# Loads of the state-space parameters by 32 partitions, and modulations of the up stage as fp32 matmuls by quarters

## The chip, the cores and the metric

The kernel runs on one core of a Trainium2 chip. Its five engines each work through their own list of instructions in order: TensorE (PE; PEld are its weight loads), VectorE (DVE), ScalarE (ACT), GpSimd (POOL) and SyncE (SP), which here issues nearly all DMAs. The metric is the device time of one execution in microseconds; the median of three runs stands for a kernel. One further execution is profiled, and all rows below come from it.

## The reference, cut to what matters

Two layers work on 512 latent and 256 context tokens of width 1024. Layer 0 mixes by attention, layer 1 by a state-space recurrence; a convolutional feed-forward network follows each.

```
m = split(silu(c) @ w_mod[i] + b_mod[i], 6)        # w_mod[i]: 1024 x 6144, all fp32
h = rms_norm(x, g_pre) * (1 + m[1]) + m[0]         # shift and scale, also before the FFN
x = x + m[2] * rms_norm(mixer(h), g_post)          # gate
dt = exp(log_step); lb = exp(lam * dt)             # per direction, group (64) and state (64)
bb = ((lb - 1) / lam) * b                          # b: 64 x 16 complex numbers per group
a = conv3(h @ w_up); ffn = (silu(gate) * val) @ w_down      # w_up: 1024 x 5632
```

The modulations m are needed once for c (latent) and once for c_ctx (context): two rows of 1024 numbers per unit, where a unit is one of the six parts of one layer.

## The kernel before, in words

Products of the model run on TensorE in three passes, high times high, high times low and low times high (`mm3`, lines 145 to 147). So each weight tile of 128x1024, loaded by SP into one of five raw buffers, is split: ScalarE makes the high half (line 108), VectorE the low one (line 109). `Weights` loads the tiles in the order of a plan; a raw buffer comes free when its reader has done with it. Instructions are ordered on each engine by a scheduler that works on its own estimate of times, so the order on an engine is not that of the source.

Attention (about 165 to 385 us) runs beside two other things. The modulations of two groups are summed on TensorE, with the weights read from their raw buffers (`mods_mm`, line 227, 32x512 outputs). And `ssm_tables` makes the tables of the state-space layer: it loads lambda, the log step and B with `by_dg` (line 1105), two loads of 64 partitions for each parameter, then the signs (128 numbers, line 1120), and VectorE negates these (`sg2`, line 1122) for the last table. The exponential of the log step (`exp`, lines 1071 to 1082) is small work on VectorE.

The up stage of layer 0 (`ffn_up`, about 445 to 890 us) takes 22 pairs of w_up tiles. Per pair TensorE fills PSUM banks (`up`), ScalarE applies one tap of the convolution (line 870) and VectorE two (line 874), which frees the banks. Beside this, VectorE builds the state-space matrices (PT and QT, lines 1243 to 1245) that TensorE transposes (pP, line 1262) or multiplies (pK, line 1291) into one of two PSUM banks with the tag "aux". And `mods_ahead` makes five units of layer 1's modulations, eight w_mod tiles each: with c as the factor of a partition, VectorE multiplies and adds into an SBUF sum (lines 297, 299), or ScalarE multiplies (line 293) and GpSimd adds (line 295). At the end of a unit TensorE sums over partitions with a matrix of ones (line 306). The first two units are made for latent and context tokens, the other three for latents alone. The sixth unit is made in the same way in the up stage of layer 1 (`ffn1`, about 1395 to 1530 us).

Of the kernel before, what the change touches and what calls it, by code (L numbers as in the profile page):

```python
# [9 lines left out]
FT = mybir.dt.float32  # L10
# [9 lines left out]
P = 128  # L20
D = 1024
# [110 lines left out]
class Kernel:  # L132
# [137 lines left out]
    def mods_ahead(self, psum, pool, units, lcs):  # L270
# [3 lines left out]
        ones = pool.tile([P, 32], FT, name="ones")  # L274
        nc.gpsimd.memset(ones, 1.0)
        n = 64 * lcs
        for l, grp, m in units:
            b = self.small.tile([P, 512], FT, name="mbias", tag="mbias", bufs=1)[:n]
            g = self.small.tile([P, 512], FT, name="mgain", tag="mgain", bufs=1)[:n]
            name = {(0, 1): "g_pre_mix", (1, 0): "g_post_mix", (2, 0): "g_pre_ffn", (2, 1): "g_post_ffn"}.get((grp, m))  # L280
            for lc in range(lcs):
                c = slice(64 * lc, 64 * lc + 64)
                nc.sync.dma_start(b[c], dap(I["b_mod"], l * 6144 + grp * 2048 + m * D, [[512, 2], [0, 32], [1, 512]]))
                if name:
                    nc.sync.dma_start(g[c], dap(I[name], l * D, [[512, 2], [0, 32], [1, 512]]))
            accs = [pool.tile([P, D], FT, name=f"macc{i}", tag=f"macc{i}", bufs=1) for i in range(lcs)]
            for k in range(KD):
                w = self.W.take()
                for lc in range(lcs):
                    a, c = accs[lc], self.cT[:, k, lc:lc + 1]  # L290
                    if lc == lcs - 1 and (lc or k % 2):
                        o = w if k else a
                        nc.scalar.activation(o, w, AF.Copy, scale=c)  # L293
                        if k:
# [7 lines left out]
            p = psum.tile([P, 512], FT, name="pm", tag="aux", bufs=2)  # L302
            for lc in range(lcs):
                for j in range(2):
                    q = 64 * lc + 32 * j
                    nc.tensor.matmul(p[q:q + 32], ones, accs[lc][:, j * 512:(j + 1) * 512], start=True, stop=True)
            v.tensor_tensor(b, p[:n], b, op=OP.add)
# [6 lines left out]
            for lc in range(lcs):  # L314
                nc.gpsimd.dma_start(dap(self.mdram[l, grp], lc * 2048 + m * D, [[512, 2], [1, 512]]),
                                    b[64 * lc:64 * lc + 64:32, :])
            if l and (grp, m) in ((1, 1), (2, 0)):
                p = psum.tile([P, 4, P], FT, name="pmc", tag="aux", bufs=2)
                for i in range(4):
                    nc.tensor.transpose(p[:, i, :64], b[:, i * P:(i + 1) * P], self.ident[:64, :64])  # L320
                v.tensor_copy(self.cols[1, 1][:, 0, grp - 1, :].rearrange("p (q b) -> p q b", b=4),
                              p[:, :, 0:33:32].rearrange("p b q -> p q b"))
# [643 lines left out]
    def ffn0(self):  # L966
# [25 lines left out]
        def mods():  # L992
            for i, units in enumerate(UP_MODS[0]):
                mp = self.pool(f"mods{i}", "right")
                for j, _ in enumerate(self.mods_ahead(ps, mp, units, 2 - i)):
                    if j == KD * len(units) - 1:
                        mp.release()
                    yield
# [821 lines left out]
```

## Time and profile before

| what | value |
|---|---|
| median of three runs | 1720.65 us (1717.9 to 1722.14) |
| profiled execution, its time | 1725.43 us |
| profiled execution, its span | 1723.6 us |
| busy: PE, DVE, ACT, POOL | 1531.6, 1132.2, 776.6, 252.3 us |
| mean granted clock of TensorE | 0.951 |

The span runs from the first instruction to the last; the time is 1.8 us more. Busy time is the union of an engine's instructions. The granted clock is given as a share of full speed: 0.5 is 1.2 GHz and 1.0 is 2.4 GHz. A matmul of fp32 operands leaves two records in the trace, one of the split operands leaves one. Matmuls are pipelined, so the step from one start to the next, not the duration, is what one costs in a stream.

### The profile page before, as it was taken

Reading aid. Unit: us, or ns where it says so; the run is one execution under the profiler, and the core shown is the slowest. Engines: PE = TensorE matmul, PEld = TensorE weight load, DVE = VectorE, ACT = ScalarE, POOL = GpSimd, SP = SyncE. Lnnn points to the kernel's source line nnn. Section 1 sums busy time; section 2 is a strip of 40 time slices with the busy share of each in tenths; the row PEclk is TensorE's granted clock in tenths of the full one; section 3 lists DMA queues with packets and bytes.
Section 4 is the critical chain, followed back from the end, with each engine's and each line's share of the span. In section 5 each row is a group of like instructions: output and inputs, shape, how many; then the busy total and the mean of one; then the engine's idle time right before and its main releaser. Section 6 shows DMA issues by size and latency. Waiting matters only on the chain.

```text
span 1723.6 us, 22808 instructions
## 1 busy us (share of the span) xinstructions
PE 1531.6 (89%) x8376; PEld 1230.2 (71%) x8376; DVE 1132.2 (66%) x2084; ACT 776.6 (45%) x1470; POOL 252.3 (15%) x203
## 2 busy tenths in 40 slices
PE   5999389999899898988999989673789999999997
PEld 2775258888778777866788877433578888888886
DVE  4653378758988988887863367689835656565334
ACT  4464167756544343332333345565544534443322
POOL 0111050000130402020200010448311001100000
PEclk8999599999999999999999999896899999999999
DMA  9424162158355647585754278664443334432421
GB/s 302 138 75 149 72 208 68 50 182 277 103 174 155 175 142 203 146 206 157 214 133 150 96 244 252 174 187 156 132 151 104 117 98 147 135 94 96 166 74 49
DMA packets 218483, 256.38 MB, mean 149 GB/s; under 512 B 19420, under 2 KB 169572, under 8 KB 217732
## 3 DMA queue, kind: packets, MB, share of 16 engines
q1 hardware_dynamic: 217940, 254.85, 48.8%
q8 instruction: 66, 1.08, 0.3%
q14 instruction: 45, 0.37, 0.1%
q0 software_dynamic: 384, 0.07, 0.0%
q10 hardware_dynamic: 48, 0.01, 0.0%
HBM read 216.95 MB, written 34.80 MB: 146 GB/s over the span
## 4 chain that ended last, share of the span: by engine, by line
PE 64%; DVE 16%; DMA 10%; ACT 5%; issue 3%; SPq 3%; POOL 0%; DVEq 0%; ACTq 0%; POOLq 0%
PE up L145 8%; PE up L146 8%; PE up L147 8%; PE dn L146 5%; PE dn L145 5%; PE dn L147 5%; DMA wraw<-in_w_mod 2%; PE acc L145 2%; PE acc L146 2%; PE acc L147 2%; DMA tab<-tabd 2%; DVE whl L109 2%; PE glu L145 2%; PE glu L147 1%; PE glu L146 1%
## 5 line engine op out<-in xcount | busy, mean ns | idle before, releaser
L109 DVE TENSOR_TENSOR whl<-wraw,whl 128x1024 fp32r<-128x1024 f32 x202 | 259.8, 1291 | 178.3 <-ACT whl L108 176.8
L108 ACT ACTIVATE whl<-wraw 128x1024 fp32r<-128x1024 f32 x206 | 216.9, 1056 | 203.2 <-PE dn L147 137.8
L145 PE MATMUL up<-b,whl 128*128 128x256 f32 (+1 forms) x728 | 248.5, 343 | 27.8 <-DVE h L874 15.9
L146 PE MATMUL up<-b,whl 128*128 128x256 f32 (+1 forms) x728 | 246.7, 340 | 0.1
L147 PE MATMUL up<-b,whl 128*128 128x256 f32 (+1 forms) x728 | 246.4, 340 | 0.0
L145 PEld LDWEIGHTS up<-b,whl 128*128 128x128 f32 x728 | 140.8, 194 | 51.8 <-issue 31.1
L146 PE MATMUL dn<-whl,hs 128*128 128x512 f32 x440 | 171.8, 393 | 4.8 <-DVE whl L109 4.7
L147 PE MATMUL dn<-whl,hs 128*128 128x512 f32 x440 | 170.9, 392 | 0.0
L145 PE MATMUL dn<-whl,hs 128*128 128x512 f32 x440 | 170.3, 392 | 0.5 <-ACT hs L934 0.5
L146 PEld LDWEIGHTS up<-b,whl 128*128 128x128 f32 x728 | 141.1, 194 | 18.9 <-issue 4.3
L147 PEld LDWEIGHTS up<-b,whl 128*128 128x128 f32 x728 | 141.0, 194 | 16.7 <-issue 2.4
L146 PE MATMUL up<-c,whl 128*128 128x512 f32 (+1 forms) x384 | 142.5, 373 | 0.1
L147 PE MATMUL up<-c,whl 128*128 128x512 f32 (+1 forms) x384 | 141.8, 371 | 0.0
L145 PE MATMUL up<-c,whl 128*128 128x512 f32 (+1 forms) x384 | 139.4, 372 | 1.0 <-DVE c L355 1.0
L295 POOL TENSOR_TENSOR macc<-macc,wraw 128x1024 f32<-128x1024 f32 x30 | 81.1, 2704 | 312.1 <-ACT wraw L293 246.2
L874 DVE SCALAR_TENSOR_TENSOR ga<-up,cw,ga 128x511 f32<-128x511 f32 (+1 forms) x132 | 86.3, 655 | 60.3 <-ACT ga L870 59.3
L870 ACT ACTIVATE ga<-up,cw 128x512 f32<-128x512 f32 (+1 forms) x66 | 46.5, 705 | 139.0 <-PE up L147 133.3
L146 PEld LDWEIGHTS dn<-whl,hs 128*128 128x128 f32 x440 | 82.6, 188 | 24.3 <-DVE whl L109 6.5
L874 DVE SCALAR_TENSOR_TENSOR h<-up,cw,h 128x511 f32<-128x511 f32 (+1 forms) x132 | 86.2, 653 | 19.0 <-ACT h L870 18.5
L145 PEld LDWEIGHTS dn<-whl,hs 128*128 128x128 f32 x440 | 82.7, 188 | 18.9 <-ACT hs L934 0.9
L147 PEld LDWEIGHTS dn<-whl,hs 128*128 128x128 f32 x440 | 82.7, 188 | 17.9
L145 PEld LDWEIGHTS up<-c,whl 128*128 128x128 f32 x384 | 71.4, 188 | 15.1 <-DVE c L355 1.5
(358 smaller groups left out, 3151.3 us busy)
## 6 DMA issues: line engine op xcount, KB each, us to landing
wraw<-in_w_up SPq DMA_DIRECT2D x88, 512.0 KB
wraw<-in_w_mod SPq DMA_DIRECT2D x80, 512.0 KB
wraw<-in_w_down SPq DMA_DIRECT2D x66, 512.0 KB
wraw<-in_w_o SPq DMA_DIRECT2D x24, 512.0 KB
Pt<-Pd SPq DMA_DIRECT2D x24, 512.0 KB
Pt<-Qd SPq DMA_DIRECT2D x32, 384.0 KB
wm<-in_w_mod SPq DMA_DIRECT2D x16, 512.0 KB
Pd<-Pb SPq DMA_DIRECT2D x16, 512.0 KB
```

The source lines that it names most:

```text
L108: nc.scalar.activation(w[:, 0], r, AF.Copy)
L109: e.tensor_tensor(w[:, 1], r, w[:, 0], op=OP.subtract)
L145: nc.tensor.matmul(out, a[0], b[0], start=start, stop=False)
L146: nc.tensor.matmul(out, a[0], b[1], start=False, stop=False)
L147: nc.tensor.matmul(out, a[1], b[0], start=False, stop=stop)
L295: nc.gpsimd.tensor_tensor(a, a, o, op=OP.add)
L870: nc.scalar.activation(o, acc, AF.Identity, scale=c[:, 1:2], bias=c[:, 3:4])
L874: nc.vector.scalar_tensor_tensor(x, acc[:, a + s:b + s], c[:, tap:tap + 1], x, op0=OP.mult, op1=OP.add)
```

## The change

The loads of `by_dg` are cut by direction, so that each covers 32 partitions with one run per partition. The log step is loaded first, then lambda, the signs and B. The negation of the signs is written beside the rows that use it. In `mods_ahead`, the sums on VectorE, ScalarE and GpSimd give way to fp32 matmuls: for each w_mod tile, four matmuls whose moving operand is a quarter of 256 columns and whose output lies in one of the four groups of 32 partitions of one PSUM bank ("aux"), which is held through the eight tiles. Bias and gain are loaded by quarters too. The pools for the SBUF sums go.

```
-        for h in range(2):
-            nc.sync.dma_start(t[64 * h:64 * h + 64], dap(I[name], 32 * h * n, [[G * n, 2], [n, 32], [1, n]]))
+            for d in range(2):
+                p0 = 64 * h + 32 * d
+                nc.sync.dma_start(t[p0:p0 + 32], dap(I[name], (G * d + 32 * h) * n, [[n, 32], [1, n]]))
...
+        self.by_dg(ls, "ssm_log_step", 1)
         self.by_dg(lam[:, 0], "ssm_lambda_re", NS)
         self.by_dg(lam[:, 1], "ssm_lambda_im", NS)
-        self.by_dg(ls, "ssm_log_step", 1)
+        nc.sync.dma_start(sg, self.I["signs"])
         self.by_dg(bt[:, 0].rearrange("p n c -> p (n c)"), "ssm_b_re", NS * GC)
         self.by_dg(bt[:, 1].rearrange("p n c -> p (n c)"), "ssm_b_im", NS * GC)
-        nc.sync.dma_start(sg, self.I["signs"])
-        v.tensor_scalar(sg2, sg, -1.0, None, op0=OP.mult)
...
         self.A = self.cst.tile([P, 2, 64], FT, name="lamT")
+        v.tensor_scalar(sg2, sg, -1.0, None, op0=OP.mult)
...
+            for q in range(4):
+                c = slice(32 * q, 32 * q + 32)
+                nc.sync.dma_start(b[c], dap(I["b_mod"], ... + 256 * q, [[0, 32], [1, 256]]))
+            acc = psum.tile([P, 512], FT, name="macc", tag="aux", bufs=2)[:, :256]
             for k in range(KD):
                 w = self.W.take()
-                for lc in range(lcs):
-                    a, c = accs[lc], self.cT[:, k, lc:lc + 1]
-                    if lc == lcs - 1 and (lc or k % 2):
-                        nc.scalar.activation(o, w, AF.Copy, scale=c)
-                        nc.gpsimd.tensor_tensor(a, a, o, op=OP.add)
-                    elif k == 0:
-                        v.tensor_scalar(a, w, c, None, op0=OP.mult)
-                    else:
-                        v.scalar_tensor_tensor(a, w, c, a, op0=OP.mult, op1=OP.add)
+                for q in range(4):
+                    nc.tensor.matmul(acc[32 * q:32 * q + 32], self.cT[:, k, :], w[:, 256 * q:256 * q + 256],
+                                     start=(k == 0), stop=(k == KD - 1))
-            for lc in range(lcs):
-                for j in range(2):
-                    nc.tensor.matmul(p[q:q + 32], ones, accs[lc][:, j * 512:(j + 1) * 512], start=True, stop=True)
```

The order on SP before, in the attention stage: the loads of the parameters, with the gain of the feed-forward norm ahead of them and the signs last.

```order
L220 DMA mgain<-in_g_post_ffn 64x1x512
L1105 DMA lam<-in_ssm_lambda_re 64x1x64 x2
L1105 DMA lam<-in_ssm_lambda_im 64x1x64 x2
L1105 DMA ls<-in_ssm_log_step 64x1x1 x2
L1105 DMA bt<-in_ssm_b_re 64x1x1024
L215 DMA mbias<-in_b_mod 128x1x512
L1105 DMA bt<-in_ssm_b_re 64x1x1024
L1105 DMA bt<-in_ssm_b_im 64x1x1024 x2
L1120 DMA sg<-in_signs 128x1
```

The same place on SP in the changed kernel:

```order
L220 DMA mgain<-in_g_post_ffn 64x1x512
L1086 DMA ls<-in_ssm_log_step 32x1 x4
L1086 DMA lam<-in_ssm_lambda_re 32x64 x4
L1086 DMA lam<-in_ssm_lambda_im 32x64 x2
L215 DMA mbias<-in_b_mod 128x1x512
L1086 DMA lam<-in_ssm_lambda_im 32x64 x2
L1099 DMA sg<-in_signs 128x1
L1086 DMA bt<-in_ssm_b_re 32x1024 x4
L1086 DMA bt<-in_ssm_b_im 32x1024 x4
```

The signs moved from behind the four loads of B to a place ahead of eight; 13 issues stand between the gain and the signs, in place of 11.

On VectorE before, in the same stage, the first exponential (edt), a row maximum of attention (sm) and the negation of the signs (sg):

```order
L1079 SCALAR_TENSOR_TENSOR edt<-edt 128x1
L652 TENSOR_SCALAR sm<-sm 128x1
L1079 SCALAR_TENSOR_TENSOR edt<-edt 128x1 x3
L1122 TENSOR_SCALAR sg_2149<-sg 128x1
L1080 TENSOR_SCALAR edt<-edt 128x1
L1082 TENSOR_TENSOR edt<-edt,eidt 128x1
L655 RECIPROCAL sm<-sm 128x1
```

On VectorE in the changed kernel:

```order
L634 TENSOR_REDUCE sm<-s 128x1
L1058 SCALAR_TENSOR_TENSOR edt<-edt 128x1
L1164 TENSOR_SCALAR sg_2669<-sg 128x1
L1132 RECIPROCAL dz<-dz 128x64
L635 TENSOR_SCALAR sm<-sm 128x1
L1058 SCALAR_TENSOR_TENSOR edt<-edt 128x1
L1059 TENSOR_SCALAR edt<-edt 128x1
```

Though the source has the negation far below, the scheduler puts it at nearly the same place, two small operations earlier.

On TensorE before, in the up stage of layer 0, the end of the second unit: the sums with ones (pm) between two passes of products (up).

```order
L145 MATMUL up<-b_7_3591,whl_5278 128x256
L146 MATMUL up<-b_7_3591,whl_5278 128x256
L147 MATMUL up<-b_7_3591,whl_5278 128x256
L306 MATMUL pm<-macc_4825,ones 32x512 x2
L306 MATMUL pm<-macc_4826,ones 32x512 x2
L146 MATMUL up<-b_2_3578,whl_5486 128x512
```

On TensorE in the changed kernel, earlier in the same stage, the quarters (macc) of two w_mod tiles, the second one torn, and one half of a job's transposes (pP):

```order
L147 MATMUL up<-b_7_3593,whl_4938 128x512
L287 MATMUL macc<-wraw_4941,cT 32x256 x4
L287 MATMUL macc<-wraw_5059,cT 32x256 x3
L1243 MATMUL pP<-ident,PT 128x128 x4
L145 MATMUL up<-b_0_3586,whl_5109 128x512
```

The fourth quarter of wraw_5059 stands 75 rows further on. Before, nothing of the modulations stood on TensorE but the sums with ones, and a job's eight transposes stood together in most places; now they stand in fours while a unit holds its bank.

## Rows read from the trace of the kernel before

**Rows 1.** Stretches: us, busy us (count) by engine, clock, DMA share, GB/s

```profile
175.00:190.00 15.00, 10.29 (x39) 8.03 (x37) 6.07 (x34) 5.65 (x15) 1.57 (x5) 0.55 0.21 68
190.00:210.00 20.00, 0.03 (x1) 0.00 (x0) 0.21 (x2) 0.00 (x0) 0.00 (x0) 0.63 0.12 48
210.00:260.00 50.00, 42.56 (x257) 28.04 (x258) 38.23 (x93) 29.71 (x58) 24.05 (x34) 0.91 0.60 184
445.00:890.00 445.00, 405.03 (x2431) 333.68 (x2430) 375.28 (x515) 175.03 (x274) 75.57 (x35) 0.97 0.60 167
1395.00:1530.00 135.00, 135.00 (x596) 110.82 (x595) 81.04 (x97) 56.73 (x71) 10.22 (x5) 1.00 0.43 127
```

**Rows 2.** Timeline of VectorE: start, us, instruction, idle before and its releaser

```profile
184.06 0.15 DVE L1071 TENSOR_SCALAR edt<-ls 128x1 f32<-128x1 f32 x1 [4.50 <-DMA ls<-in_ssm_log_step]
...
209.79 0.15 DVE L1122 TENSOR_SCALAR sg<-sg 128x1 f32<-128x1 f32 x1 [22.18 <-DMA sg<-in_signs]
```

**Rows 3.** Timeline of SP's DMA issues from 174 to 196

```profile
174.12 0.54 SPq L220 DMA_DIRECT2D mgain<-in_g_pre_ffn  x1
...
176.58 3.16 SPq L1105 DMA_DIRECT2D lam<-in_ssm_lambda_im  x2
179.79 2.60 SPq L1105 DMA_DIRECT2D ls<-in_ssm_log_step  x2
182.49 0.50 SPq L1105 DMA_DIRECT2D bt<-in_ssm_b_re  x1
...
191.02 4.73 SPq L1120 DMA_DIRECT2D sg<-in_signs  x1
```

**Rows 4.** Groups by line in 445:890: busy us, mean ns, idle before, releasers

```profile
L145 PE MATMUL up<-b,whl 128*128 128x512 f32 (+1 forms) x664 | 231.1, 350 | 27.8 <-DVE h L874 15.9 <-DVE ga L874 10.9 <-ACT Pb L1263 0.9
...
L109 DVE TENSOR_TENSOR whl<-wraw,whl 128x1024 fp32r<-128x1024 f32 x42 | 58.9, 1402 | 0.5 <-ACT whl L108 0.5
...
L299 DVE SCALAR_TENSOR_TENSOR macc<-wraw,cT,macc 128x1024 f32<-128x1024 f32 x23 | 35.1, 1528 | 16.1 <-DMA wraw<-in_w_mod 14.3 <-POOL macc L295 1.8
...
L295 POOL TENSOR_TENSOR macc<-macc,wraw 128x1024 f32<-128x1024 f32 x26 | 71.5, 2749 | 185.1 <-ACT wraw L293 119.1 <-DVE Ks L1299 56.0 <-DVE macc L299 5.1
```

**Rows 5.** Timelines of VectorE and GpSimd from 456 to 461

```profile
456.38 0.29 DVE L1337 TENSOR_TENSOR lpt<-lpw 128x128 f32<-128x128 f32 x1
...
457.11 2.33 DVE L1340 TENSOR_TENSOR lpt<-lpw 128x128 f32<-128x128 f32 x1
...
460.29 1.21 DVE L109 TENSOR_TENSOR whl<-wraw,whl 128x1024 fp32r<-128x1024 f32 x1
...
456.88 2.40 POOL L295 TENSOR_TENSOR macc<-macc,wraw 128x1024 f32<-128x1024 f32 x1 [8.26 <-ACT wraw L293]
```

**Rows 6.** Timeline of TensorE around fp32 matmuls with 32 output partitions

```profile
47.81 1.92 PE L538 MATMUL acc<-wm,cT 128*32 128x256 f32 x28
...
157.04 0.40 PE L146 MATMUL acc<-whl,a 128*128 128x512 f32 x1
157.27 0.40 PE L147 MATMUL acc<-whl,a 128*128 128x512 f32 x1
157.60 1.07 PE L227 MATMUL macc<-wraw,cT 128*32 128x512 f32 x8
...
158.93 0.39 PE L146 MATMUL acc<-whl,a 128*128 128x512 f32 x1
...
1513.92 1.05 PE L306 MATMUL pm<-macc,ones 128*32 128x512 f32 x4
```

**Rows 7.** Groups by line in 115:255, where TensorE reads w_mod itself

```profile
L227 PE MATMUL macc<-wraw,cT 128*32 128x512 f32 x128 | 26.6, 620 | 3.8 <-DMA wraw<-in_w_mod 2.6 <-issue 1.3
```

**Rows 8.** Waits in 445:890: who for whom, us in total, times, longest

```profile
ACT wraw L293 <- DMA wraw<-in_w_mod: 45.5, 10, 13.3
...
DVE macc L299 <- DMA wraw<-in_w_mod: 14.3, 6, 4.2
```

**Rows 9.** Weight loads of the same matmuls: ns min/median/max, first and last start

```profile
L227 PEld LDWEIGHTS macc<-wraw,cT x128: 106/109/154, 118.7 to 250.6; 128*32 128x32 f32 x128
```

More of the change, by code (lines that the diff above doesn't have):

```diff
@@ L268, in mods_end, with mods_ahead @@
                         pv[:, 64 * m + lc:64 * m + lc + 33:32, :])
-    def mods_ahead(self, psum, pool, units, lcs):
+    def mods_ahead(self, psum, units, lcs):
         nc, v, I = self.nc, self.nc.vector, self.I
-        ones = pool.tile([P, 32], FT, name="ones")
-        nc.gpsimd.memset(ones, 1.0)
-        n = 64 * lcs
         for l, grp, m in units:
-            b = self.small.tile([P, 512], FT, name="mbias", tag="mbias", bufs=1)[:n]
-            g = self.small.tile([P, 512], FT, name="mgain", tag="mgain", bufs=1)[:n]
+            b = self.small.tile([P, 512], FT, name="mbias", tag="mbias", bufs=1)[:, :256]
+            g = self.small.tile([P, 512], FT, name="mgain", tag="mgain", bufs=1)[:, :256]
@@ L280, in mods_ahead @@
             name = {(0, 1): "g_pre_mix", (1, 0): "g_post_mix", (2, 0): "g_pre_ffn", (2, 1): "g_post_ffn"}.get((grp, m))
[L281 to L283 removed]
+            for q in range(4):
+                c = slice(32 * q, 32 * q + 32)
+                nc.sync.dma_start(b[c], dap(I["b_mod"], l * 6144 + grp * 2048 + m * D + 256 * q, [[0, 32], [1, 256]]))
@@ L284, in mods_ahead @@
                 if name:
[L285 to L286 removed]
+                    nc.sync.dma_start(g[c], dap(I[name], l * D + 256 * q, [[0, 32], [1, 256]]))
+            acc = psum.tile([P, 512], FT, name="macc", tag="aux", bufs=2)[:, :256]
             for k in range(KD):
                 w = self.W.take()
[L289 to L299 removed]
+                for q in range(4):
+                    nc.tensor.matmul(acc[32 * q:32 * q + 32], self.cT[:, k, :], w[:, 256 * q:256 * q + 256],
+                                     start=(k == 0), stop=(k == KD - 1))
@@ L300, in mods_ahead @@
                 if k < KD - 1:
                     yield
-            p = psum.tile([P, 512], FT, name="pm", tag="aux", bufs=2)
-            for lc in range(lcs):
-                for j in range(2):
-                    q = 64 * lc + 32 * j
-                    nc.tensor.matmul(p[q:q + 32], ones, accs[lc][:, j * 512:(j + 1) * 512], start=True, stop=True)
-            v.tensor_tensor(b, p[:n], b, op=OP.add)
+            v.tensor_tensor(b, acc, b, op=OP.add)
             if (grp, m) in ((0, 1), (2, 0)):
@@ L314, in mods_ahead @@
             for lc in range(lcs):
-                nc.gpsimd.dma_start(dap(self.mdram[l, grp], lc * 2048 + m * D, [[512, 2], [1, 512]]),
-                                    b[64 * lc:64 * lc + 64:32, :])
+                nc.gpsimd.dma_start(dap(self.mdram[l, grp], lc * 2048 + m * D, [[256, 4], [1, 256]]), b[lc:P:32, :])
             if l and (grp, m) in ((1, 1), (2, 0)):
[L318 to L322, printed above, removed]
+                p = psum.tile([P, 2, P], FT, name="pmc", tag="aux", bufs=2)
+                for i in range(2):
+                    nc.tensor.transpose(p[:, i], b[:, i * P:(i + 1) * P], self.ident)
+                v.tensor_copy(self.cols[1, 1][:, 0, grp - 1, :].rearrange("p (q b) -> p q b", b=2),
+                              p[:, :, 0:P:32].rearrange("p b q -> p q b"))
             yield
@@ L993, in mods @@
             for i, units in enumerate(UP_MODS[0]):
[L994 to L998, printed above, removed]
+                yield from self.mods_ahead(ps, units, 2 - i)
         def rows_of(pool, lc):
@@ L1745, in ffn1 @@
         self.bits = True
-        def mods():
-            mp = self.pool("mods2", "right")
-            for j, _ in enumerate(self.mods_ahead(ps, mp, UP_MODS[1][0], 1)):
-                if j == KD - 1:
-                    mp.release()
-                yield
-        self.ffn_up(1, ((self.act, LAT),), "right", lambda: iter(()), [0] * NF, mods())
+        self.ffn_up(1, ((self.act, LAT),), "right", lambda: iter(()), [0] * NF, self.mods_ahead(ps, UP_MODS[1][0], 1))
         self.actp.release()
```

6 lines of the change are left out of this document (3 added, 3 removed).

## The prediction, made before the changed kernel was run

> **What bounds the kernel now.** I read the stretches first, because the change touches three stages with different limits [rows 1]. In 190:210 nothing runs: TensorE is busy 0.03 of 20 us, VectorE 0.21, and the DMA engines show a share of 0.12 at 48 GB/s. In 445:890, the first layer's up stage, TensorE is busy 405.0 of 445 us and VectorE 375.3, so two engines are near their limit and hinder each other; the mean granted clock is 0.97. In 1395:1530, the second layer's up stage, TensorE is busy all 135 us at 1.00: there each added matmul is paid in full.
>
> The hole at 190 is one wait. VectorE's timeline [rows 2] shows the negation of the signs at 209.79 after 22.18 us of idling for the load of the signs; the row maxima and the low halves of the probabilities, for which TensorE and ScalarE wait, stand behind it on VectorE. The queue of DMA issues [rows 3] says why: the signs are issued last, at 191.02, behind the two B tables (64 partitions x 4 KB in each of four loads, 1 MB), and 0.12 of 16 engines at 48 GB/s is two engines: 1 MB takes 21 us there.
>
> In 445:890 the wait that TensorE has is for VectorE: of the idle time before the first products of a pass, 27.8 us, the taps of the convolution (h and ga) ended 26.8 [rows 4].
>
> **Part one, the parameters.** Two edits: the order of the loads (log step, lambda, signs, then B) and their form (20 loads of 32 partitions for ten of 64). The negation stands later in the source, but on VectorE it still stands among the operations of the first exponential, so it is still waited for; what counts is when the signs land. Ahead of them the queue now has 4 + 8 loads and one of b_mod, 13 issues from 175.25 on. At the price of an unhindered issue, 0.50 us (the bt row at 182.49), with some 0.05 between them, the signs are issued at 182.4; the log step took 2.2 us from its second issue (179.79 + 2.60 - 0.50 = 181.89) to VectorE's start at 184.06 [rows 2, 3], so they are there at 184.6. The gains of the feed-forward norms, two loads of 128 KB in the old form (the first at 174.12), still stand ahead: 256 KB at 48 GB/s is 5.3 us from 176, so no part that shares their engines lands before 181.3. The log step then comes 2.7 us earlier than 184.06, and VectorE, which needed 187.61 - 184.06 = 3.55 us from there to the negation, is at it at 184.9. It passes it at about 185 in place of 209.8: 24.8 us, all on the path, since TensorE's products of values wait for VectorE. B is wanted 20 us after the stall and has 1 MB to move with the queue free, so nothing else is late next. The clock gives a little more: it was 0.55 before the hole and 0.91 in the 50 us after [rows 1], 18% of them, 9 us, at the lower level of 1.2 GHz; I count nothing for it beyond rounding. Bounds: if the 13 issues cost what the two of lambda_im cost, 1.58 us each, the signs land at 198 and 12 us are gained; if neither wait is left, 22.2 + 4.5 = 27. I take -25, since issues were slow only where two engines were backed up.
>
> The Trainium skill, "DMA: Bandwidth & Descriptors" (Why a DMA increments its semaphore by 16 and not by 1), says that a load runs on the largest number of engines up to 16 that divides the slowest dimension of both sides: two for the old form, 16 for the new. The share of 0.12 agrees for the old form; no row has the new one. By that rule B would need an eighth of its 21 us, some 3 us, an estimate; the sum above does not use it, as the signs now stand ahead of B.
>
> **Part two, the first up stage.** Five of the six units (40 loads of w_mod) are here. Gone from VectorE: 23 multiply-adds, 35.1 us, and five multiplies; from GpSimd 71.5 us of adds [rows 4]; from ScalarE the copies scaled by c. More goes with GpSimd's adds: while one ran (456.88, 2.40 us) a 128x128 VectorE product took 2.33 us, beside 0.29 for the same shape just before [rows 5], and the splits in this stage average 1402 ns [rows 4], against 1.21 us for the one at 460.29, with GpSimd at rest. So VectorE falls from 375 to 320 to 330 of 445 us.
>
> Added on TensorE: four matmuls of 32x256 in fp32 per load, eight records. In [rows 6] 28 such records take 1.92 us, 69 ns each, where records with twice the columns average 620 [rows 7]: the four quarters run together. The price with its seams comes from the same kind with 512 columns: from 157.27 to 158.93 two ordinary steps of 0.23 and eight records, so these cost 1.20 us, two slots of 0.43 and 0.33 for leaving and re-entering the stream. Quarters of 256 columns need two slots of 0.215, 0.43 us a piece. The order of the changed program has the 40 loads in 28 places, seven of them torn in two, so 47 pieces: 47 x 0.43 + 28 x 0.32 = 29.2 us. Removed are the five sums with ones, like the row at 1513.92 (1.05 us busy against 1.07 for the eight records), 1.18 us each: 5.9. TensorE has 23.3 us more to do.
>
> Against this stand the 40 us in which it idled, and the clock: 0.03 of 445 is 13 us lost at most to stretches at 1.2 GHz, which follow idle time. Of these 53 I take three quarters, 40 us, as recovered: the waits for h and ga (26.8) are for an engine that now has 50 us less to do; waits for the state-space products, built on VectorE from tables that come by DMA, remain in part. Bounds: 10 (VectorE was late for its own bursts) and 53.
>
> New waits. TensorE reads the loads itself and stands in line until they land: in the earlier stage where it does so already, 32 loads cost 2.6 us [rows 7], so 40 cost 3.3; the upper bound is what ScalarE and VectorE waited for them here, 45.5 + 14.3 [rows 8]. And the sums now hold one of two PSUM banks through eight loads, so the transposes of a job come in halves of four with one bank: in [rows 4] a wait for such an eviction cost 0.9, once; 32 evictions would be 28 us, but products stand between the halves in the new order; I take 2. On SP the five units issue 32 loads of bias and gain in place of 11, 21 x 0.5 us, beside weights that are issued ahead. Sum: 23.3 + 5 - 40 = -12.
>
> **Part three, the second up stage.** One unit: eight loads, in 12 places and 12 pieces: 12 x (0.43 + 0.32) = 9.0, less 1.2 for its sum with ones: +8. VectorE and ScalarE have slack there, so relief buys nothing. Bounds +5 and +10.
>
> **The sum** is made against the profiled execution: 1725.43 us, 1.8 above its span. -25 - 12 + 8 = -29 gives 1696.4. The median of the runs is 1720.65, 4.8 lower; the forecast is 1692.
>
> A rule that speaks against the change: the Trainium skill, "TensorE: Matmul & The Clock Gate" (The mechanism, under Part 3), says that a weight load overlaps running matmuls only where the row groups differ, and here all four quarters use all rows. By it 48 x 8 loads of 109 ns [rows 9] would come on top. The row of 28 records in 1.92 us contradicts it, since their loads alone would be 3.1 us.
>
> **Rivals.**
> The holes close wholly: quarters are put where TensorE would have waited for a tap, and all 53 us return: 23.3 - 53 = -30 in the first up stage, 1674 in all. For it: VectorE at 325 of 445. Against: the state-space jobs still come in bursts.
> TensorE inherits the waits for w_mod: a stalled matmul holds every product behind it, where ScalarE's stall held little. With the 60 us of [rows 8], 23 + 60 - 40 = +43, in all +26: 1747, slower. It decides from 32 us of such waits on. For it: VectorE, as full as TensorE, did wait 14.3. Against: the 2.6 us of [rows 7].
> Weight loads are exposed: 48 x 8 x 0.109 = 42 us, 1734, slower; against it the 28 records.
> The signs land no earlier, because the issues back up: -12 + 8, 1717, no change. Against: the signs are ahead of B.
> VectorE paces the up stage as before, and only some 28 of 53 us come back: its gain is nil, 1704.
>
> **How the numbers follow.** The forecast gets 0.58 (1682 to 1703), the closed holes 0.17, the inherited waits 0.08, the exposed loads 0.02, the late signs 0.07, no gain in the up stage 0.08. The range from 1670 to 1716 leaves out the slower cases and the lowest end. A measurement tells 0.3%, 5 us, from no change. Faster: 0.58 + 0.17 + 0.08 and a little of the late signs, 0.85; same 0.05; slower 0.10.
>
> **What the profile after would show.** The signs' wait under 2 us and no empty stretch after 190; the up stage 10 to 15 us shorter, VectorE under 340 us in it, TensorE's busy share over 0.95, records of the quarters starting four together; the second up stage 8 us longer. The forecast is wrong if TensorE's quarters wait for w_mod by more than 20 us in all, if transposes wait for evictions, or if the negation still idles VectorE by ten.

## The result, and the profile after

The changed kernel takes 1697.97 us (median of 4 runs, 1692.19 to 1698.61) against 1720.53 for the kernel before on the same chip (now of 4 runs too, 1717.9 to 1722.14): ratio 0.9863, 95% interval 0.9838 to 0.9888. The forecast was 1692 with a range of 1670 to 1716, so the total fell where it was expected. The stages inside it did not, and most of what follows is on that.

The two profiled executions lie on opposite sides of their medians: 1725.43 before is 4.9 over, 1692.19 after is 5.8 under. Between the profiles the span shrinks by 33.2 us (1723.6 to 1690.4), between the medians the time shrinks by 22.6, or 1.4%. Stages can be read from the profiles alone, so the table uses them, and a few microseconds of any stage are scatter. Each border is the first or last instruction of a kind on TensorE.

| Stretch | Before | After | Change | Forecast |
|---|---|---|---|---|
| start to the last product of values | 358.7 | 340.2 | -18.5 | -25 |
| first up stage (first to last product with b) | 472.6 | 442.4 | -30.2 | -12 |
| down stage and state-space entry, to the first output product (py) | 269.5 | 268.6 | -0.9 | 0 |
| first py to the second layer's first up product | 176.7 | 184.7 | +7.9 | 0 |
| second up stage | 249.7 | 257.9 | +8.2 | +8 |

How large that scatter is can be read from the kernels of the experiments below that share the code of a stretch. Seven profiles with the change's loads end the first stretch 13.7 to 18.5 us earlier than the kernel before (mean 16.8), so the changed kernel's own 18.5 is the upper end. The first up stage takes 466.3 to 474.7 us in four profiles with the old modulations (mean 470.3) and 440.6 to 444.7 in four with the new (mean 442.7): a gain of 27.6 between the means.

The page after, busy time by engine and the chain that ended last:

```profile
PE 1543.8 (91%) x8724; PEld 1228.7 (73%) x8724; DVE 1060.1 (63%) x2052; ACT 745.8 (44%) x1438; POOL 169.8 (10%) x170
...
PE 75%; DVE 11%; DMA 6%; ACT 4%; issue 2%; SPq 1%; POOL 0%; DVEq 0%; ACTq 0%; POOLq 0%
```

Stretches after, with the columns of [rows 1]; the third row is the whole first up stage, the last lies in the second:

```profile
175.00:190.00 15.00, 7.64 (x26) 5.78 (x24) 5.65 (x29) 3.69 (x10) 0.90 (x3) 0.50 0.35 99
190.00:210.00 20.00, 17.57 (x105) 12.31 (x106) 14.81 (x58) 15.55 (x30) 4.63 (x16) 0.87 0.39 120
...
407.40:849.80 442.40, 435.25 (x2943) 358.32 (x2941) 327.18 (x543) 161.07 (x274) 3.98 (x7) 1.00 0.61 177
...
1353.30:1488.30 135.00, 135.00 (x620) 104.82 (x619) 71.17 (x88) 50.09 (x62) 0.10 (x1) 1.00 0.41 121
```

The empty stretch after 190 [rows 1] is full: TensorE is busy 17.57 of 20 us. But 175:190 is now poorer (7.64 us in place of 10.29): part of the hole has moved ahead. In the first up stage the clock is 1.00 and VectorE, 397 us busy over that whole stage before, is at 327.

VectorE's timeline after, the two places that answer to [rows 2]:

```profile
182.36 0.15 DVE L1050 TENSOR_SCALAR edt<-ls 128x1 f32<-128x1 f32 x1 [3.64 <-DMA ls<-in_ssm_log_step]
...
189.14 0.15 DVE L1164 TENSOR_SCALAR sg<-sg 128x1 f32<-128x1 f32 x1 [3.50 <-DMA sg<-in_signs]
```

SP's issues after, against [rows 3]:

```profile
174.41 1.82 SPq L1086 DMA_DIRECT2D ls<-in_ssm_log_step  x4
176.28 5.58 SPq L1086 DMA_DIRECT2D lam<-in_ssm_lambda_re  x4
181.90 0.88 SPq L1086 DMA_DIRECT2D lam<-in_ssm_lambda_im  x2
...
184.64 0.36 SPq L1099 DMA_DIRECT2D sg<-in_signs  x1
185.10 1.76 SPq L1086 DMA_DIRECT2D bt<-in_ssm_b_re  x4
```

The negation passes at 189.14 in place of 209.79, 20.7 us earlier, and not 25: four loads of lambda held the queue for 5.58 us (the four ahead of them took 1.82, about 0.45 each), so the signs were issued at 184.64, and they took 4.5 us from there to VectorE's start. It is the place in the queue that costs, not what the loads carry. In form_only below, four loads of lambda stand first and take 1.96 us, and the four behind them are held:

```profile
174.15 1.96 SPq L1107 DMA_DIRECT2D lam<-in_ssm_lambda_re  x4
176.16 5.00 SPq L1107 DMA_DIRECT2D lam<-in_ssm_lambda_im  x4
```

In ten profiles with loads of 32 partitions the first four small loads behind the gains take 1.8 to 2.1 us and the second four 5.0 to 5.8, until 180 to 183. That the gains, 256 KB in the old form, hold the queue that long fits these times, but no run moved them away.

Groups of the first up stage after, against [rows 4]:

```profile
L145 PE MATMUL up<-b,whl 128*128 128x256 f32 (+1 forms) x728 | 243.4, 337 | 2.6 <-DVE h L857 2.5
...
L109 DVE TENSOR_TENSOR whl<-wraw,whl 128x1024 fp32r<-128x1024 f32 x45 | 54.9, 1219 | 28.0 <-ACT whl L108 25.6 <-PE macc L287 2.4
...
L287 PE MATMUL macc<-wraw,cT 128*32 128x256 f32 x320 | 25.1, 385 | 0.0
```

TensorE's idle time before the first products of a pass, nearly all of it waits for taps, fell from 27.8 to 2.6 us; a split on VectorE takes 1219 ns on average in place of 1402; and the quarters wait for w_mod by 0.0 us.

### The profile page after: what moved, and what is told of

It is laid out like the page before. It is cut to its first block, busy times and chain, and to the rows that moved or that the text cites. A ratio compares the mean times of both kernels' runs of the same rounds, so it can differ in the third digit from the quotient of the medians.

```text
span 1690.4 us, 23335 instructions
## 1 busy us (share of the span) xinstructions
PE 1543.8 (91%) x8724; PEld 1228.7 (73%) x8724; DVE 1060.1 (63%) x2052; ACT 745.8 (44%) x1438; POOL 169.8 (10%) x170
## 4 chain that ended last, share of the span: by engine, by line
PE 75%; DVE 11%; DMA 6%; ACT 4%; issue 2%; SPq 1%; POOL 0%; DVEq 0%; ACTq 0%; POOLq 0%
PE up L145 12%; PE up L147 11%; PE up L146 11%; PE dn L145 5%; PE dn L146 5%; PE dn L147 5%; PE acc L145 2%; PE acc L147 2%; PE acc L146 2%; PE glu L145 2%; PE glu L147 2%; PE glu L146 2%; PE macc L287 2%; DMA wm<-in_w_mod 1%; DVE t L1428 1%
## 5 line engine op out<-in xcount | busy, mean ns | idle before, releaser
L109 DVE TENSOR_TENSOR whl<-wraw,whl 128x1024 fp32r<-128x1024 f32 x202 | 250.2, 1243 | 210.9 <-ACT whl L108 207.5
L145 PE MATMUL up<-b,whl 128*128 128x256 f32 (+1 forms) x728 | 243.4, 337 | 2.6 <-DVE h L857 2.5
L147 PE MATMUL up<-b,whl 128*128 128x256 f32 (+1 forms) x728 | 241.4, 335 | 0.5 <-DVE whl L109 0.5
L146 PE MATMUL up<-b,whl 128*128 128x256 f32 (+1 forms) x728 | 241.6, 334 | 0.0
L145 PEld LDWEIGHTS up<-b,whl 128*128 128x128 f32 x728 | 136.9, 189 | 26.4 <-issue 6.1
L146 PEld LDWEIGHTS up<-b,whl 128*128 128x128 f32 x728 | 137.3, 189 | 16.3 <-issue 2.0
L147 PEld LDWEIGHTS up<-b,whl 128*128 128x128 f32 x728 | 136.4, 189 | 16.5 <-issue 2.2
L853 ACT ACTIVATE ga<-up,cw 128x512 f32<-128x512 f32 x66 | 46.5, 705 | 151.5 <-PE up L147 149.8
L145 PEld LDWEIGHTS dn<-whl,hs 128*128 128x128 f32 x440 | 83.0, 189 | 18.6 <-ACT ga L853 0.4
L145 PEld LDWEIGHTS up<-c,whl 128*128 128x128 f32 x384 | 71.3, 188 | 18.0 <-issue 4.5
L147 PEld LDWEIGHTS up<-c,whl 128*128 128x128 f32 x384 | 72.3, 188 | 13.4 <-issue 0.4
```

Of the source, the lines that this page charges most:

```text
L109: e.tensor_tensor(w[:, 1], r, w[:, 0], op=OP.subtract)
L145: nc.tensor.matmul(out, a[0], b[0], start=start, stop=False)
L146: nc.tensor.matmul(out, a[0], b[1], start=False, stop=False)
L147: nc.tensor.matmul(out, a[1], b[0], start=False, stop=stop)
L853: nc.scalar.activation(o, acc, AF.Identity, scale=c[:, 1:2], bias=c[:, 3:4])
```

## The experiments

All ratios are against runs of the kernel before made with them on the same chip (medians 1722.3 to 1723.6).

**The two parts apart.** `p1_only` is the kernel before with the change's by_dg and ssm_tables; `p2_only` the changed kernel with by_dg and ssm_tables of before. The core of each, as it differs from the kernel before:

```diff
# p1_only (its ssm_tables: as in the change)
-            self.nc.sync.dma_start(t[64 * h:64 * h + 64], dap(self.I[name], 32 * h * n, [[G * n, 2], [n, 32], [1, n]]))
+            for d in range(2):
+                p0 = 64 * h + 32 * d
+                self.nc.sync.dma_start(t[p0:p0 + 32], dap(self.I[name], (G * d + 32 * h) * n, [[n, 32], [1, n]]))
...
# p2_only (its mods_ahead: as in the change)
-                    if lc == lcs - 1 and (lc or k % 2):
...
+                    nc.tensor.matmul(acc[32 * q:32 * q + 32], self.cT[:, k, :], w[:, 256 * q:256 * q + 256],
...
```

> The parameters' part alone: 20 loads of 32 partitions, signs ahead of B, modulations as in the kernel before. Theory: the attention stage gives the same 18.5 us as in the changed kernel (last products of values to the first of w_o moves from 358.6 to 340 us), and the first up stage (472.6 us) and the second (249.6) stay as they were, since the two parts do not touch: about 1702, ratio 0.989. Rival (the parts share work: the earlier signs only move VectorE's backlog): attention gives under 10 us and the time is above 1711.

> The modulations' part alone, parameters loaded as in the kernel before, signs last. Theory: the hole of 22 us at 190 us stays, the first up stage is 30 us shorter (472.6 to about 442), the second 8 longer; without the 8 us that the changed kernel lost between the last down product and the first up product of the second layer: 1699, with them 1707. Rival (the gain in the up stage came from the earlier tables of part one): the up stage is shorter by under 12 us and the time is 1716 or more.

Measured: part one alone 1705.96, ratio 0.9897 (0.9881 to 0.9912); part two alone 1713.52, 0.9942 (0.992 to 0.9964). Stages of their profiles against the kernel before: part one -18.4 in attention, +2.1 in the first up stage, +1.9 between py and the second layer's first up product, 0 in the second up stage; part two -0.7, -32.0, +7.5, +8.3. No sign that the parts touch: -17.6 and -10.1 in the medians add up to -27.7, the changed kernel has -22.6, and the intervals cover the difference. The gain in the up stage needs nothing of part one. (order_only and form_only below, whose up stage has the old modulations, are 6.3 and 5.0 us shorter there; that is the scatter named above, and it bounds what a difference of a few microseconds in that stage can tell.) The loss of 8 us ahead of the second layer comes with part two here; more on it below.

**Order or form.** `order_only` changes the order of the loads and keeps two loads of 64 partitions each; `form_only` cuts the loads into four of 32 and keeps the order, signs last:

```diff
# order_only, from the kernel before
+        self.by_dg(ls, "ssm_log_step", 1)
         self.by_dg(lam[:, 0], "ssm_lambda_re", NS)
         self.by_dg(lam[:, 1], "ssm_lambda_im", NS)
-        self.by_dg(ls, "ssm_log_step", 1)
+        nc.sync.dma_start(sg, self.I["signs"])
...
# form_only, from the kernel before: the lines of by_dg that p1_only shows
```

> Only the order of the loads (log step, lambda, signs, then B; the negation late), in the old form of 64 partitions. Theory that the order does it: attention gives 15 to 22 us, time 1699 to 1706, though the loads still run at 48 GB/s on two engines. Rival that the form does it: the signs still wait for two engines that are backed up with 256 KB of gains and the small loads, the hole shrinks by under 8 us and the time is 1713 or more.

> Only the form of the loads (20 of 32 partitions), in the old order: B ahead, signs last. Theory that the order does it: the signs are still the last of 21 issues; if B takes what it took, nothing is gained, 1720. Rival that the form does it: B no longer runs on two engines, its 1 MB takes 3 to 6 us in place of 21, the wait for the signs falls from 22 us to under 8, and the time is 1704 to 1709. Between them (issues backed up at 1.6 us each): signs some 10 us earlier, 1710.

Measured: order alone 1708.04, 0.9914 (0.9887 to 0.994), attention -16.7; form alone 1706.05, 0.9894 (0.9878 to 0.9911), attention -16.2. Neither "the order does it" nor "the form does it": each does it alone, and 16.7 and 16.2 cannot be told from the 13.7 to 18.5 of the profiles that have both. (The time of order_only lies 2 us above its theory's range.) With the form alone the signs are issued last, at 190.55, and yet nobody waits for them: VectorE's timeline in form_only,

```profile
189.90 0.15 DVE L1071 TENSOR_SCALAR edt<-ls 128x1 f32<-128x1 f32 x1 [6.03 <-DMA ls<-in_ssm_log_step]
...
194.34 0.15 DVE L1124 TENSOR_SCALAR sg<-sg 128x1 f32<-128x1 f32 x1
```

since B moves on more engines; its wait is now for the log step, 6.03 us. The same ten microseconds, with B under way, in form_only and then in the kernel before (columns of [rows 1]):

```profile
184.00:194.00 10.00, 1.82 (x5) 1.34 (x6) 3.68 (x18) 2.03 (x5) 0.00 (x0) 0.63 0.52 130
```

```profile
184.00:194.00 10.00, 5.36 (x20) 4.04 (x20) 3.30 (x20) 2.32 (x6) 0.41 (x2) 0.77 0.16 52
```

130 GB/s in place of 52. The Trainium skill, "DMA: Bandwidth & Descriptors" (Why a DMA increments its semaphore by 16 and not by 1), lets a 32-partition load use 16 engines; the shares of 0.52 and 0.16 agree that it uses many more than two. These ten microseconds are a mean: in form_only the transfers are over by 192, and the two microseconds from 186 show a share of 1.05 at 205 GB/s, where the kernel before shows 0.13 at 49 to 53 GB/s from 192 to 196. At eight times the share the rate is four times as high, and not eight. With the order alone B still crawls (49 to 53 GB/s from 188 to 196), but the wait moved to GpSimd, 6.1 us for the last of B, and the stretch is as short as with the form alone.

**What is left of the hole.** `early` loads the log step and the signs into tiles of their own, ahead of the query projection in the source. On SP these loads stand far earlier still, at 17 to 21 us, some 155 us before VectorE uses them:

```diff
+        self.ls = self.cst.tile([P, 1], FT, name="ls")
+        self.sg = self.cst.tile([P, 1], FT, name="sg")
+        self.by_dg(self.ls, "ssm_log_step", 1)
+        nc.sync.dma_start(self.sg, I["signs"])
         jobs = self.mods_jobs(ps, MODS[:1], "acc", NT)
```

> The changed kernel with the log step and the signs loaded into tiles of their own before the query projection, some 60 us ahead. Theory: of the attention stage's hole only VectorE's waits for these two loads are left, 3.6 and 3.5 us; both go, the stage gives 25 in place of 18.5 and the time is 1691. Rival: lambda, issued in the same 5.6 us of backed-up queue, or the probabilities from ScalarE are late next, the stage gives under 3 us more and the time is 1695 to 1698.

Measured: 1689.23, 0.9813 (0.9789 to 0.9836), as the theory has it in the time. Attention gives 22.3 in this profile, and 25.8 in early_u6 below, whose code is the same up to there; seven profiles of kernels that share the changed kernel's code up to there give 13.7 to 18.5. So the two waits were worth some 4 to 12 us, 7.3 between the means, and the 7.1 that they show lies in that. They are not the end: in early_u6 VectorE stands at 181.75 for the next load in the queue,

```profile
181.75 0.41 DVE L1161 TENSOR_SCALAR dz<-lam,edt 128x128 f32<-128x128 f32 x1 [3.58 <-DMA lam<-in_ssm_lambda_im]
```

**What held the first up stage.** Five kernels vary the work around TensorE there. `pool_adds` puts 26 additions back on GpSimd, `dve_adds` 23 multiply-adds on VectorE, `all_adds` everything that VectorE, ScalarE and GpSimd did before, each beside the quarters:

```diff
# pool_adds, in the loop over k
+                if pool and k == 0:
+                    v.tensor_scalar(a, w, 1.0, None, op0=OP.mult)
+                elif pool and (lcs == 2 or k % 2):
+                    nc.gpsimd.tensor_tensor(a, a, w, op=OP.add)
...
# dve_adds, in place of the last two lines
+                elif pool and (lcs == 2 or k % 2 == 0):
+                    v.scalar_tensor_tensor(a, w, self.cT[:, k, 0:1], a, op0=OP.mult, op1=OP.add)
# all_adds, behind the quarters
+                for lc in range(lcs if pool else 0):
+                    a, c = accs[lc], self.cT[:, k, lc:lc + 1]
+                    if lc == lcs - 1 and (lc or k % 2):
+                        o = w if k else a
+                        nc.scalar.activation(o, w, AF.Copy, scale=c)
+                        if k:
+                            nc.gpsimd.tensor_tensor(a, a, o, op=OP.add)
...
```

`sums_cut` leaves out TensorE's quarters but for a unit's first load, `halves` makes two pieces of 32 x 512 of the four:

```diff
# sums_cut
-                for q in range(4):
+                for q in range(0 if k else 4):
...
# halves
-                for q in range(4):
-                    nc.tensor.matmul(acc[32 * q:32 * q + 32], self.cT[:, k, :], w[:, 256 * q:256 * q + 256],
+                for q in range(2):
+                    nc.tensor.matmul(acc[32 * q:32 * q + 32], self.cT[:, k, :], w[:, 512 * q:512 * q + 512],
...
```

> The changed kernel with 26 additions of 128 x 1024 on GpSimd in the first up stage, as many as the kernel before had there, into a tile that nothing reads (and five starts of it on VectorE). Theory that what VectorE lost there was mostly the neighbourhood of GpSimd's additions: VectorE's operations beside them are stretched again by some 40 us, TensorE waits for taps again, and the first up stage grows from 442 to between 455 and 472 us; time 1711 to 1728. Rival that the relief was VectorE's own 23 multiply-adds: the stage stays within 5 us of 442 and the time is 1698 to 1703.

> The changed kernel with VectorE's 23 multiply-adds of 128 x 1024 back in the first up stage, into a tile that nothing reads; none on GpSimd. Theory (VectorE's own load held TensorE up, GpSimd's additions only a little, 9 us): the stage grows from 442 us by 10 to 30, to between 452 and 472. Rival (with GpSimd at rest VectorE has room for 35 us more, and what held TensorE up was the two together, or ScalarE): it stays within 5 us of 442 and the time is 1698 to 1703.

> The changed kernel with all that VectorE, ScalarE and GpSimd did for the first up stage's modulations in the kernel before added again beside TensorE's quarters, into tiles that nothing reads. Theory (the stage won 53 us by taking this work off and paid some 20 on TensorE): the holes come back and the stage grows from 442 to between 480 and 500 us; time 1735 to 1755. Rival (the holes went for another reason, such as the order in which the stage's work now stands): it stays under 460 and the time under 1716.

> The changed kernel with TensorE's quarters for the first of each unit's eight loads only, so that the modulations' sums lack seven eighths; the loads of w_mod stay. Theory (TensorE paces the stage, its work there is paid in full): 35 of 40 pieces of 0.63 us and their seams go, 22 to 27 us: 442 falls to 415 to 420; the second up stage falls from 258 to 250. Rival (VectorE is close behind, and paces it once TensorE has less to do): the first stage stays above 430.

> The changed kernel with the up stages' modulations as two pieces of 32 x 512 in place of four of 32 x 256. Theory (pieces of different columns run side by side, so a load costs by the columns of one piece): two slots of 0.43 us per load in place of two of 0.215: 0.43 x 40 = 17 us more in the first up stage (442 to 459), 3.4 more in the second (258 to 261). Rival (only two pieces run side by side, or the leaving of the stream is the whole price): both stages as in the changed kernel, within 4 us. Between the last down product and the second layer's first up product its instructions stand in the order of the kernel before, so there it should not lose the 8 us that the changed kernel lost (first state-space output to first up product 177 us in place of 184.7). In all 1710 by the theory, 1690 by the rival.

Times: pool_adds 1705.42, 0.9894 (0.9868 to 0.992); dve_adds 1689.74, 0.9818 (0.9794 to 0.9842); all_adds 1729.32, 1.0038 (1.0024 to 1.0053); sums_cut 1675.3, 0.9729 (0.9711 to 0.9747); halves 1700.24, 0.9871 (0.9849 to 0.9892). The stage by itself (columns of [rows 1]), first the kernel before:

```profile
425.90:898.50 472.60, 432.63 (x2657) 360.61 (x2656) 396.83 (x572) 188.02 (x302) 75.57 (x35) 0.97 0.59 166
```

pool_adds:

```profile
409.50:861.00 451.50, 438.61 (x2939) 359.73 (x2938) 356.85 (x548) 160.96 (x274) 73.20 (x33) 0.99 0.60 172
```

dve_adds:

```profile
412.20:856.40 444.20, 438.92 (x2938) 357.58 (x2936) 353.66 (x571) 161.69 (x274) 3.96 (x7) 1.00 0.61 176
```

all_adds:

```profile
411.20:888.70 477.50, 447.72 (x2943) 365.11 (x2941) 396.89 (x571) 190.10 (x302) 77.04 (x33) 0.97 0.57 163
```

sums_cut:

```profile
408.10:847.90 439.80, 420.68 (x2681) 356.70 (x2680) 323.34 (x544) 159.05 (x275) 3.97 (x7) 0.99 0.63 182
```

halves:

```profile
407.90:856.10 448.20, 446.26 (x2772) 353.12 (x2770) 329.37 (x543) 162.02 (x274) 3.82 (x7) 1.00 0.60 174
```

Read the length of the stretch (472.60 in the first row) and VectorE's busy time (396.83). From the changed kernel's 442.4 us, GpSimd's additions cost 9.1 and VectorE's own multiply-adds, 29.4 us of them here, cost 1.8; both together with ScalarE's copies cost 35.1 (of these numbers 1.8 lies inside the scatter of 440.6 to 444.7), and VectorE is back at 396.89, the kernel before's number to 0.1 us. pool_adds falls between its theory (455 or more) and its rival (447 or less), dve_adds on its rival's side, all_adds on its theory's, 2.5 us short of it. The last speaks against the order of the stage's work as what closed the holes. So the old work held the stage up, but not by its sum: with VectorE 354 and 357 us busy the stage grows by 2 and 9, with 397, and the copies beside it, by 35. The two single additions raise VectorE's busy time by 29.7 and 26.5; together it rises by 69.7, 13.5 more. Splits on VectorE hold 8.3 of these (all_adds and then dve_adds):

```profile
L109 DVE TENSOR_TENSOR whl<-wraw,whl 128x1024 fp32r<-128x1024 f32 x45 | 63.1, 1402 | 12.3 <-ACT whl L108 12.1 <-PE pP L1260 0.3
```

```profile
L109 DVE TENSOR_TENSOR whl<-wraw,whl 128x1024 fp32r<-128x1024 f32 x45 | 54.8, 1217 | 4.7 <-ACT whl L108 4.7
```

GpSimd's additions stretch what VectorE does beside them: in pool_adds VectorE's 29.7 us more hold only 3.4 of own new work, the five starts. There it is not the splits that grow (1218 ns) but products of two SBUF operands, PT among them, while the taps, which read PSUM, take 745 ns with and without (VectorE in pool_adds, then in the changed kernel):

```profile
L1235 DVE TENSOR_TENSOR PT<-tabw,tab 128x1024 f32<-128x1024 f32 x16 | 23.8, 1490 | 12.7 <-DMA tab<-tabd 12.6
L863 DVE SCALAR_TENSOR_TENSOR ga<-up,cw,ga 128x511 f32<-128x511 f32 x44 | 32.8, 745 | 4.4 <-ACT ga L859 4.0
```

```profile
L1225 DVE TENSOR_TENSOR PT<-tabw,tab 128x1024 f32<-128x1024 f32 x16 | 19.5, 1220 | 10.8 <-DMA tab<-tabd 10.6
L857 DVE SCALAR_TENSOR_TENSOR ga<-up,cw,ga 128x511 f32<-128x511 f32 x44 | 32.8, 745 | 11.2 <-ACT ga L853 10.8
```

The Trainium skill, "SBUF — State Buffer" (SBUF: two separate sides), calls the port pair of VectorE and GpSimd an exclusive lock and no split of bandwidth, against VectorE's operations with two SBUF inputs among others; the 26 us against 69.1 us of additions agree with a lock that takes only some of VectorE's operations. Of all_adds' 35.1 us, 24 are neither of the single additions: ScalarE's 28 copies (31.5 us) were never put back alone. In all_adds they also write over the weight tile that the quarters read, so that ScalarE waits for TensorE first (7.2 us). How the 24 split between the copies, these waits and the meeting of all three stays open.

The other end is sums_cut: with 35 of 40 loads taken off TensorE its busy time falls by 14.6 us, and the stage by only 2.6, which is hardly more than the scatter. TensorE then idles 18.6 us (the sum of its idle times above 0.3 us), 13.3 of them before state-space products (pK, pP), whose operands VectorE builds from tables that come by DMA. The four longest of its waits in sums_cut (sum, times, longest):

```profile
PE pK L1272 <- issue: 4.3, 1, 4.3
PE pK L1272 <- DVE QT L1226: 3.6, 4, 1.2
PE up L145 <- DVE ga L857: 3.6, 3, 1.5
PE pP L1243 <- DVE PT L1226: 3.4, 1, 3.4
```

So the theory "paid in full" falls for this stage and the rival's number (above 430) holds: the quarters fill holes that TensorE has anyway. That VectorE paces the stage without them is shown only as far as these waits go: it is busy 323 of 440 us. halves confirms the holes from above: its pieces cost TensorE 17 us more (40.1 against 23.1, summed over the pieces by the starts of the steps around them, as below; its busy time grows by 11.0), its idle time falls to 1.9, and the stage grows by 5.8 in place of the 17 that its theory had.

In the second up stage, where TensorE waits for 1.1 us in all, prices are paid as worked out. TensorE's timeline there, the changed kernel and then halves:

```profile
1384.91 0.39 PE L147 MATMUL up<-c,whl 128*128 128x512 f32 x1
1385.22 0.62 PE L287 MATMUL macc<-wraw,cT 128*32 128x256 f32 x4
1385.78 0.50 PE L145 MATMUL up<-c,whl 128*128 128x512 f32 x1
1386.12 0.40 PE L146 MATMUL up<-c,whl 128*128 128x512 f32 x1
```

```profile
1393.79 0.39 PE L147 MATMUL up<-c,whl 128*128 128x512 f32 x1
1394.11 1.05 PE L287 MATMUL macc<-wraw,cT 128*32 128x512 f32 x4
1395.09 0.50 PE L145 MATMUL up<-c,whl 128*128 128x512 f32 x1
1395.43 0.39 PE L146 MATMUL up<-c,whl 128*128 128x512 f32 x1
```

From the step before to the second step after stand 1.21 us in the first, less two ordinary steps of 0.227: 0.76 for the piece. All twelve pieces of the stage cost 0.75 to 0.77, whether they hold 2, 4, 6 or 8 records; halves' ten cost 1.18 each, and its stage takes 260.5 us. The time of halves, 1700.24, lies half-way between its theory (1710) and its rival (1690). The forecast had 0.75, and 0.43 more for twice the columns. sums_cut gets 7.9 us of the 8.2 back with seven of eight loads.

**The second up stage's unit in the old way, and both edits together.** `unit6_old` is the changed kernel with the old mods_ahead kept under another name for that one unit, `early_u6` the same with the early loads:

```diff
-        self.ffn_up(1, ((self.act, LAT),), "right", lambda: iter(()), [0] * NF, self.mods_ahead(ps, UP_MODS[1][0], 1))
+            for j, _ in enumerate(self.mods_old(ps, mp, UP_MODS[1][0], 1)):
...
+        self.ffn_up(1, ((self.act, LAT),), "right", lambda: iter(()), [0] * NF, mods())
```

> The changed kernel with the second up stage's one unit (eight loads) made as in the kernel before, by VectorE, ScalarE and GpSimd. Theory: TensorE paces that stage without a hole, so it returns from 257.9 us to 249.6 and the time falls by 8, to 1690. Rival (what VectorE and ScalarE do for it holds the taps there too, as in the first up stage): the stage stays within 3 us of 258 and the time near 1698.

> Both edits that helped, on the changed kernel: the log step and the signs loaded ahead, and the second up stage's unit made in the old way. Theory: they touch different stages and add up, 1689 less 8 to 13: 1676 to 1681, under both kernels. Rival: what one gives is lost again where the stages meet, 1685.

Measured: unit6_old 1684.91, 0.9777 (0.9754 to 0.98), the theory's side and 5 us below it; its one profile is of an execution of 4635 us, so its stages are not read. early_u6 1679.86, 0.975 (0.9728 to 0.9771): 18 us under the changed kernel and 42 under the kernel before, the fastest kernel that makes all sums (sums_cut, at 1675.3, leaves most of them out). In its profile the second up stage is 249.7 us, as the theory has it. Alone the edits gave 13 and 9 us, together 18: they add up within the intervals.

**The 8 us ahead of the second layer.** No kernel was made for this; the others show it on the way. TensorE's wait after the first py, in the changed kernel and in the kernel before:

```profile
PE py L1587 <- ACT SA L1572: 28.7, 3, 25.4
```

```profile
PE py L1606 <- ACT SA L1591: 11.7, 3, 7.4
```

ScalarE's copies of the carries (SA), for which TensorE waits there, the changed kernel and then the kernel before:

```profile
1145.12 8.31 ACT L1572 ACTIVATE SA<-B 64x512 f32<-64x512 f32 x8 [16.60 <-DVE B L1565]
```

```profile
1176.89 8.29 ACT L1591 ACTIVATE SA<-B 64x512 f32<-64x512 f32 x8 [12.36 <-DVE B L1584]
```

They come 26.7 us after the first py (1118.4) in the one, 8.9 after it (1168.0) in the other: the scheduler has put VectorE's, ScalarE's and GpSimd's instructions of this stage in another order, though no edit is near it. Stretches from first py to first product of the gated unit, and from there to the second layer's first up product, in order_only and then in p1_only:

```profile
1140.00:1194.30 54.30, 15.82 (x134) 13.37 (x134) 52.13 (x76) 22.14 (x25) 41.31 (x34) 0.58 0.27 96
1194.30:1324.50 130.20, 118.57 (x679) 93.11 (x679) 68.05 (x128) 65.72 (x110) 20.93 (x17) 0.96 0.46 144
```

```profile
1148.30:1188.60 40.30, 17.23 (x134) 14.82 (x134) 39.44 (x43) 21.33 (x23) 31.93 (x29) 0.59 0.38 132
1188.60:1327.00 138.40, 121.50 (x680) 96.69 (x679) 76.25 (x153) 65.77 (x110) 28.63 (x24) 0.93 0.43 135
```

184.5 and 178.7 us. order_only has only half of part one and yet the changed kernel's order, row by row on VectorE and ScalarE; p1_only has all of part one and the order of before. From the last down product of the first layer to the second layer's first up product the two kernels in the old order take 255.8 and 256.4 us; the eight profiles in the new order, or nearly in it, 261.7 to 264.2; three in an order close to the old one 256.7 (dve_adds), 259.3 (sums_cut) and 262.4 (halves). This is how dve_adds, with more work than the changed kernel, is not slower than it. halves speaks against the rule: forecast in the old order with 177 us from the first py to the first up product, it took 181.1. So of thirteen profiles eleven fit the rule, one lies between and one is against it. The order alone was not flipped; that it is the cause stays an inference.

## Why the prediction came out as it did

- **What bounds the kernel.** Right: the hole at 190 was the wait for the signs, and in the first up stage the other engines' work held TensorE (all_adds puts it back and the stage is 477.5 us again).
- **The signs (-25).** Right mechanism, mis-sized: 18.5 in this profile, 13.7 to 18.5 with the same loads. The step that failed is "the signs are issued at 182.4 and there at 184.6": the forecast let the gains hold two engines until 181.3 and yet took 13 issues at the unhindered 0.50 us, but the four loads of lambda_re took 5.58 us to issue, until 181.86. That put the signs at 184.64, and landing took 4.5 us, not 2.2. VectorE had come to it by 185.6 (forecast 184.9) and waited 3.5. early and early_u6, with both waits gone, give 22.3 and 25.8. The forecast also credited the order alone; the form alone does the same.
- **The first up stage (-12).** Here the rival of the closed holes came, with its -30. The price was near: the changed kernel's pieces sum to 23.1 us beside 29.2, less 5.9 for the removed sums, so some 17 in place of 23.3. The step that failed is taking three quarters of 53 us as recovered: TensorE's idle times above 0.3 us fell from 39.5 in sum to 6.9, and the 30.7 us that TensorE spent at 1.2 GHz in this stage became 3.4, worth half of the difference, 13.7. So some 46 of the 53 came back beside a price of 17, which makes the 30. The reason lies in how the sum was built: price and recovery were added as if independent, where sums_cut shows that they are the same microseconds: without most of the quarters the stage is 439.8 long, so taking the old work off gains 32.8 and the quarters cost 2.6 of it, not 17.
- **New waits (5).** Too much: 0.0 for w_mod, and the gaps that are left are 1 to 3 us each, none at an eviction.
- **The second up stage (+8).** Right, 8.2, piece by piece.
- **Not forecast.** +7.9 between py and the second layer. The forecast read the new order around its terms and took the rest as unmoved.
- **The total.** The five stretches and the rest (+0.2) give -33.2 in the profiles against -29 forecast, and -22.6 in the medians. Errors of 18 on one side and 6.5 and 8 on the other cancelled: the total is no proof of the terms. Of what the profile was to show, VectorE under 340 us (327) and TensorE's share over 0.95 (0.98) came; the signs' wait under 2 us (3.5) and 10 to 15 us in the up stage (30) did not. None of the three signs of being wrong came.
- **Rivals.** TensorE did not inherit w_mod's waits, and weight loads stayed hidden (twelve pieces of 0.76 us with up to eight loads of 109 ns [rows 9]). "No gain in the up stage" is far off.

## What to carry to other kernels

Work put on an engine that has holes is not priced by its duration alone: make one run without it and one with it doubled, as sums_cut and halves, before calling it expensive. Pieces of work that look harmless one at a time (9 and 2 us here) can cost 35 together with a third. Where a scheduler orders the program, compare the order of stages that the edit does not touch as well, and read experiments stage by stage; a total mixes the edit with the order.

## Not expected of the hardware

- A load cut from 64 partitions into twos of 32 moved B at 130 in place of 52 GB/s, and up to 205 in two microseconds, at a share of 1.05. Behind the two loads of gains the first four small loads took 1.8 to 2.1 us to issue and the next four 5.0 to 5.8, whether they carried lambda's real or imaginary part.
- A piece of fp32 matmuls with 32 output partitions costs 0.75 to 0.77 us whether 2 or 8 records stand in it, and 1.18 with twice the columns.
- 26 additions on GpSimd (69 us) made VectorE's other work 26 us longer; with 23 multiply-adds on VectorE and ScalarE's copies beside them it was some 13 more.
